# A two-layer decoder step: one chain for both heads, the inverse's last step on two tiles, conditioning by transposes, a new order

## Chip, cores and metric

The kernel runs on one core of one Trainium2 chip. The metric is the device time of one execution in microseconds (us), lower is better; the median of three runs is given. A profile is one execution recorded on the chip.

## The reference, cut to what matters

One inference step of two layers, for a prompt of 512 tokens and for 8 samples of 8 new tokens each (with 1024 cached tokens), D = 1024. All is float32.

```python
def modulate(x, gain, shift, scale):
    return rms_norm(x, gain) * (1 + scale[:, None, :]) + shift[:, None, :]
# layer 0: shift, scale, gate = split(c @ ada_w + ada_b, 3)
proj = modulate(x, ...) @ w_in                  # 1024 -> 6176
q, k, v = causal_conv(qkv), then silu           # 8 q/k heads, 16 v heads of 128
# gated delta rule, chunk by chunk (WY form), per v head
a = tril((k * beta) @ k.T * decay, -1)
t_inv = solve_triangular(eye + a, eye)
u = t_inv @ (v * beta);  w = t_inv @ (k * beta * exp(g))
for each chunk:
    v_new = u - w @ s
    o = (q * exp(g)) @ s + (q @ k.T * decay) @ v_new
    s = s * exp(g_last) + (k * exp(g_last - g)).T @ v_new
o = rms_norm(o) * silu(z);  x = x + gate * (o @ w_out)
# shared k, v = modulate(x, ...) @ w_kv, rms norm and partial rotary on k
# layer 1: differential attention of q over cached and new k, v; silu(z) gate;
#          output projection; x = x + gate * y
```

The conditioning vectors `shift`, `scale`, `gate` come from `c @ ada_w + ada_b` for nine vectors `c`: one of the prompt, eight of the samples.

## The kernel before, in words

All 576 tokens (512 + 64) are held as columns, in two halves of 288; a feature block of 128 is the partition dimension. The big projections split each float32 operand into a high and a low part (`whi`, `wlo`, `hhi`, `hlo`, type fp32r) and sum three products, each 128 x 128 weights by 288 columns. Those are the rows with 128x288 in the profile. Other products are plain fp32, which the profile shows as two records each.

The program has three parts, each written out by a small list scheduler at build time:

- `Opening` loads `x`, the first weights and the first conditioning weights, sums squares, and runs the first products as soon as conditioning arrives (`modulated`).
- `Weave` (the first layer, `phase_a`) keeps a set of generators. Each generator yields the engine it needs next (E or L for TensorE, A for ScalarE (ACT), D or S for VectorE (DVE), P or Q for GpSimd (POOL)), an assumed cost, and the conditions to wait for; then it issues its instructions. `Weave.drive` takes the one that can start first by its own model, and among equals the one of the lowest rank. A `Room` is a buffer that is taken and left. The order that comes out is pinned per engine (`woven`), in the first layer for PE, ACT, DVE and POOL (`PINNED`). Where the model sees TensorE idle for long, it fills in small bf16 products (`fill`). Loads are assumed to land `LATE` after their modelled end.
- `Second` (the second layer, `phase_b`) is a `Weave` too, with SP's queue (most of the loads and stores) pinned as well.

The first layer works on 8 groups `g`, one q/k head and two v heads (`hh` = 0, 1) each. TensorE's projections (`weave_proj`, rank 1000, so they take what the others leave) run ahead of the groups and fill the time between the groups' small steps. Within a group:

- `prep` transposes k and q, scores them, and makes the chunk matrices `ckq`; `decays` makes the decays from `gb`.
- `tinv_dve` and `tinv_pe` invert eight unit triangular 128 x 128 matrices (4 chunks by 2 heads) by blocks of 16, 32 and 64. The last step (64) is two products per matrix, with a scaled copy (`V2`) between them on ACT: block `ck` by `XA` into partitions 64 to 127, then `V2` by the lower right block of `WF` into partitions 0 to 63. The result is `WF`.
- `chain(hh)` runs the state recursion for one head: per chunk `c`, `pk` = k by the state `S` (TensorE), `r0` (DVE), `pw` = `WF` by `r0` (TensorE), `wk` = `pw` times a key scale (ACT), `pk` = `kt` by `wk` (TensorE), new `S` (DVE). `copy_w` copies `pw` plainly to `wv` (ACT) for `outputs`, which computes the chunk's outputs into the bank `po`. Both heads' `pk` and `pw` lie in one PSUM bank, `pc`.
- `output` copies `po` to `ob` and squares it in place, with sums; `post`, `head` and `sample_head` normalize, transpose and gate the output and store it (`ogd`); `gate` makes the gate from the projection with a scratch buffer (`scr`).
- `sample_gdn` and `sample_states` do the same rule for the samples, on POOL, TensorE and DVE.

Conditioning appears in three places (`Opening.modulated`, `ada_units`, `ada_mod`): `c` (32 columns, 9 used) by the weights, on four column tiles of the array at once, leaves four partial sums in four partition groups; a copy to SBUF; then a product with the 0/1 matrix `asel` (9 columns) that transposes and adds the four; then DVE adds the bias into `K.mod`.

Of the kernel before, what the change touches and what calls it, by code (L numbers as in the profile page):

```python
# [18 lines left out]
D = 1024  # L19
# [167 lines left out]
def ada_units(K, W, A):  # L187

    nc = K.nc
    for n, kt in enumerate(K.kts):  # L190
# [4 lines left out]
        for k in range(8):  # L195
# [32 lines left out]


# [3 lines left out]
class Weave:  # L233
# [6 lines left out]
    def __init__(self, K):  # L240
# [3 lines left out]
        self.port = 0.0  # L244
        self.queues, self.coming = {"S": [], "P": []}, []
        self.done, self.live = {}, []
# [5 lines left out]
    def matmul(self, **kw):  # L252
# [57 lines left out]
    def transfers(self, until):  # L310

        while True:
# [13 lines left out]
            else:  # L326
                for q in act:
                    if q[0][0] < 1e-9:
                        name = q.pop(0)[1]
                        self.done[name] = t + (SPARE if "page" in str(name[0]) else LATE), None  # L330
# [20 lines left out]
    def ready(self, w):  # L351

        eng, _, *conds = w[3]
        x, asked = 0.0, {}
        for c in [w[4]] + conds:
            if isinstance(c, Room):
                i = self.taken[c] - self.bufs[c] + asked.get(c, 0)
                asked[c] = asked.get(c, 0) + 1
                c = (0.0, None) if i < 0 else self.left.get((c, i))
            elif isinstance(c, float):  # L360
# [6 lines left out]
            x = max(x, t if e is None else t + ((0.0 if eng in ("E", "L") else 0.06) if eng and e and ENGINE[e] == ENGINE[eng] else PAD if eng in ("E", "L") else HOP))  # L367
        return x

    def drive(self):  # L370
        while self.live:
# [15 lines left out]
            eng, cost, *conds = w[3]  # L387
            pe, idle = eng in ("E", "L"), x - self.free["E"]
# [3 lines left out]
            for c in conds:  # L392
                if isinstance(c, Room):
                    self.took.append((c, self.taken[c]))
                    self.taken[c] += 1
            if pe:
                self.crowd, self.seen = max(0.0, self.crowd - DRAIN * (x - self.seen)), x
            self.advance(w)
            end = x + self.cost, eng
# [11 lines left out]
    def pin(self):  # L411
        woven(self, PINNED)
# [14 lines left out]
class Opening(Weave):  # L427
# [22 lines left out]

    def pin(self):
        woven(self, PINNED + (mybir.EngineType.SP,))
# [112 lines left out]
    def modulated(self, k):  # L565
# [15 lines left out]
        for a in range(2):  # L581
            K.mm(out=ps[:, 256 + 9 * a:265 + 9 * a], lhsT=sb[:, 128 * a:128 * a + 128], rhs=K.asel, start=True, stop=True)
        yield "D", 0.17, ("con", 1)
        v0 = VEC["ada_b"][0] + k
        nc.vector.tensor_add(out=K.mod[:, k:k + 9:8, :], in0=ps[:, 256:274].rearrange("p (a c) -> p a c", a=2),
                             in1=K.vec[:, v0:v0 + 9:8].unsqueeze(2).to_broadcast([128, 2, 9]))
# [264 lines left out]
HOP = 0.2  # L851
LATENCY = 2.3
SHARED = 0.56
LATE = 0.6
TURN = 0.085
# [24 lines left out]
KQS = 2  # L880
# [7 lines left out]
SPARE = 1.4  # L888
# [155 lines left out]
class Group:  # L1044
# [52 lines left out]
    def gate(self, hh, half, ps, room):  # L1097
# [143 lines left out]
    def prep(self):  # L1241
# [53 lines left out]
        W.set("prep1", g)  # L1295
        gbs = self.gbs
# [38 lines left out]

    def q_squares(self, pq, pz, ssk, ssq):
# [23 lines left out]
    def chunks(self):  # L1360
# [20 lines left out]
    def chain(self, hh):  # L1381
# [3 lines left out]
        h = 2 * g + hh  # L1385
        pk, pw = self.pc[:, hh, 0], self.pc[:, hh, 1]
        for c in range(4):
            vr = self.vrs[hh]
            if c:
                S = self.S[c - 1]  # L1390
                yield "E", None
# [1828 lines left out]
```

## Time and profile before

| | |
|---|---|
| median of 3 runs (lowest to highest) | 1145.55 us (1145.44 to 1146.97) |
| the profiled execution's own time | 1145.45 us |
| its span, first to last instruction | 1143.7 us |
| mean granted TensorE clock | 0.996 |
| busy: PE / weight loads / DVE / ACT / POOL | 1118.4 / 1036.8 / 697.5 / 693.5 / 439.7 us |
| DMA moved | 239.97 MB, mean 210 GB/s |
| chain that ended last, share of PE | 78% |

PE is TensorE's matmuls, PEld its weight loads. Ends of matmuls are modelled and overlap, so a matmul's own length (about 0.3 us for 288 columns) is more than the distance to the next one (about 0.13). In the timeline a row is start, length, engine, line, operation, out<-in, shape and count, with the idle time before it and what ended that in brackets. In the groups a row is busy time and mean ns of one, then the engine's idle time before it. In the waits a row is total time waited, number of waits, longest. L271, L285, L1930 and L1935 are the helpers that issue nearly every product and transpose, so tiles tell more than lines.

### The profile page before, as it was taken

The numbers are of one execution on the slowest core, as the hardware profiler recorded it, in microseconds if no ns is written. First come the engines' busy times: TensorE is split into PE (matmuls) and PEld (weight loads), VectorE is DVE, ScalarE is ACT, GpSimd is POOL, SyncE is SP. The second block draws the span as 40 slices with busy tenths as digits, with TensorE's granted clock in tenths as the row PEclk, the third lists the DMA queues.
The fourth block names the chain that finished last, engine by engine and source line by source line (L and its number), as shares of the span: only waits on it lengthen the run. The fifth ranks groups of instructions, "written<-read, shape, count | busy, mean of one in ns | idle before, by whom it ended". The sixth has DMA issues, their size and how long they took to land.

```text
span 1143.7 us, 32504 instructions
## 1 busy us (share of the span) xinstructions
PE 1118.4 (98%) x12651; PEld 1036.8 (91%) x12651; DVE 697.5 (61%) x1803; ACT 693.5 (61%) x1901; POOL 439.7 (38%) x752
## 2 busy tenths in 40 slices
PE   8999999999999999999999999999999999999998
PEld 6899999998989998998989999999998888888998
DVE  4677875777778675876733567565432557556452
ACT  4675877777767877777744424585543566665520
POOL 3443423323334333232223343188972323313341
PEclk9999999999999999999989999999999999999999
DMA  9786565667657575686777698422489988988553
GB/s 363 218 232 168 136 200 142 188 159 193 174 132 192 146 199 149 172 227 159 231 213 192 232 320 299 158 75 75 140 293 328 318 307 304 323 305 288 185 163 95
DMA packets 87644, 239.97 MB, mean 210 GB/s; under 512 B 14451, under 2 KB 28659, under 8 KB 87491
## 3 DMA queue, kind: packets, MB, share of 16 engines
q1 hardware_dynamic: 71938, 181.27, 46.1%
q0 software_dynamic: 15552, 56.63, 22.1%
q8 instruction: 100, 1.64, 0.6%
q14 instruction: 54, 0.43, 0.1%
HBM read 212.02 MB, written 25.84 MB: 208 GB/s over the span
## 4 chain that ended last, share of the span: by engine, by line
PE 78%; ACT 7%; DVE 5%; DMA 4%; issue 3%; POOL 2%; SPq 1%; POOLq 0%; ACTq 0%; DVEq 0%
PE pp L271 24%; PE pp L1930 12%; PE pc L271 7%; PE pq L1930 7%; PE px L1930 4%; PE po L1930 3%; PE pa L271 3%; PE pt L1935 3%; PE pt L271 3%; PE sc L1930 2%; PE pt L1930 2%; PE pv L1930 2%; PE ps L271 2%; DMA whi<-wall 2%; PE pt L285 1%
## 5 line engine op out<-in xcount | busy, mean ns | idle before, releaser
L271 PE MATMUL pp<-hlo,whi 128*128 128x288 f32 x592 | 171.3, 310 | 0.0
L271 PE MATMUL pp<-hhi,whi 128*128 128x288 f32 x592 | 162.7, 295 | 0.0
L2031 POOL TENSOR_TENSOR wlo<-wraw,whi 128x512 fp32r<-128x512 f32 x78 | 106.3, 1376 | 128.7 <-ACT whi L2025 117.1
L1930 PE MATMUL pp<-hhi,whi 128*128 128x288 f32 x432 | 132.9, 308 | 1.1 <-DVE x L1829 0.8
L1930 PE MATMUL pp<-hlo,whi 128*128 128x288 f32 x432 | 127.1, 295 | 0.0
L1930 PE MATMUL pp<-hhi,wlo 128*128 128x288 f32 x432 | 125.6, 295 | 0.0
L271 PE MATMUL pp<-hhi,wraw 128*128 128x288 f32 x576 | 123.7, 298 | 0.0
L271 PEld LDWEIGHTS pp<-hlo,whi 128*128 128x128 f32 x592 | 112.0, 189 | 1.8 <-issue 1.4
L271 PEld LDWEIGHTS pp<-hhi,whi 128*128 128x128 f32 x592 | 112.2, 189 | 0.4
L271 PE MATMUL pp<-hhi,wlo 128*128 128x288 f32 x592 | 104.4, 305 | 0.0
L271 PEld LDWEIGHTS pp<-hhi,wraw 128*128 128x128 f32 x576 | 94.0, 189 | 1.0 <-issue 0.4
L1134 DVE SCALAR_TENSOR_TENSOR y<-u,vec,y 128x600 f32<-128x600 f32 x96 | 80.8, 842 | 9.8 <-ACT y L1131 9.1
L1930 PEld LDWEIGHTS pp<-hhi,whi 128*128 128x128 f32 x432 | 81.4, 188 | 5.4 <-issue 4.6
L271 PEld LDWEIGHTS pp<-hhi,wlo 128*128 128x128 f32 x592 | 85.4, 190 | 0.9 <-issue 0.2
L271 PE MATMUL pp<-hlo,wraw 128*128 128x288 f32 x288 | 84.4, 314 | 0.2 <-DVE hlo L1855 0.2
L1930 PEld LDWEIGHTS pp<-hlo,whi 128*128 128x128 f32 x432 | 81.5, 189 | 0.0
L1930 PEld LDWEIGHTS pp<-hhi,wlo 128*128 128x128 f32 x432 | 80.8, 188 | 0.0
L926 POOL DMA_DIRECT2D wlo<-wall x36 | 32.3, 897 | 119.5 <-ACT wlo L921 78.3
L2490 POOL COPY pg<-ptt 1x1 int32<-1x1 int32 x128 | 27.5, 226 | 124.7 <-PE po L1930 44.8
L2025 ACT CAST whi<-wraw 128x1024 fp32r<-128x1024 f32 x45 | 47.2, 1049 | 42.9 <-PE px L1930 13.1
L1930 PE MATMUL pq<-hhi,whi 128*128 128x288 f32 x200 | 65.0, 325 | 0.6 <-ACT vch L2247 0.4
L1930 PE MATMUL pq<-hhi,wlo 128*128 128x288 f32 x200 | 58.9, 295 | 0.0
(501 smaller groups left out, 3126.9 us busy)
## 6 DMA issues: line engine op xcount, KB each, us to landing
pg<-ck SPq DMA_DIRECT2D x64, 512.0 KB, 5.5
pg<-cv SPq DMA_DIRECT2D x64, 512.0 KB, 5.3
wraw<-wall SPq DMA_DIRECT2D x49, 512.0 KB, 4.1
wraw<-wall POOLq DMA_DIRECT2D x36, 512.0 KB, 5.6
whi<-wall POOLq DMA_DIRECT2D x36, 512.0 KB, 5.5
wlo<-wall POOLq DMA_DIRECT2D x36, 512.0 KB, 5.6
araw<-ada SPq DMA_DIRECT2D x24, 512.0 KB, 4.2
araw<-ada SPq DMA_DIRECT2D x8, 1024.0 KB, 13.7
```

The lines of the kernel that those rows point to most:

```text
L271: return self.K.nc.tensor.matmul(**kw)
L285: return self.K.nc.tensor.transpose(**kw)
L926: K.nc.gpsimd.dma_start(out=lo[:], in_=src, accum_op=ALU.add)
L1134: nc.vector.scalar_tensor_tensor(out=y[:, :YW], in0=u[:, j:j + YW], scalar=cw[j], in1=y[:, :YW], op0=ALU.mult, op1=ALU.add)
L1930: return self.K.nc.tensor.matmul(**kw)
L1935: return self.K.nc.tensor.transpose(**kw)
L2025: nc.scalar.copy(out=hi[:], in_=raw[:])
L2031: (nc.vector if shared else nc.gpsimd).tensor_sub(out=lo[:, q:q + 4], in0=raw[:, q:q + 4], in1=hi[:, q:q + 4].bitcast(F32))
L2490: nc.gpsimd.tensor_copy(out=e, in_=P.ptt[0:1, i:i + 1])
```

## The change

- `chain` serves both heads: one product of k by the state with 256 columns, two DVE steps, two products with `WF`, one ACT copy of 256 columns to `wv`, two products with keys that are scaled ahead (`keys_scaled`, two POOL products of 128x512 per group, `kts`), two DVE steps. `copy_w` is gone. `outputs` does all products of a chunk in one step, after `wv`.
- The inverse's last step puts four of the eight matrices on another tile of the array, alternating: (0,64) with (0,0), then (64,0) with (0,64). A copy `X22` on ACT brings the lower right block to partitions 0 to 63 for the second four, and each copy between is split in two.
- Conditioning: the product with `asel` becomes a transpose of 128x128, and DVE adds the four groups (`grouped`: a reduction and an addition).
- The scheduler knows a `Bank`: TensorE's use waits in its model for the last use by other engines, and theirs for TensorE's. It assumes 0.1 us between engines other than TensorE (`NEAR`), longer landings for some loads (`SLACK`), half the cost for 64x64 products, and passes the cause of a wait on through steps without an engine. SP's queue is pinned in the first layer too.
- `NUDGE` shifts the rank of single steps by hand-written amounts, 260 of them, so that the order of both layers is a new one.
- `output` squares from `ob` into a junk tile and frees `po` after the copy; the gates write the tanh into their own tile; three buffers for the convolution state (`KQS`).
- Before the opening: a memset of `hhi` and eight more warming products.

The diff, cut to its core:

```diff
...
@@ -201,12 +201,19 @@
-        K.mm(out=ps[:, 128:137], lhsT=sb[:], rhs=K.asel, start=True, stop=True)
-        yield "D", 0.22
-        v0 = VEC["ada_b"][0] + kt
-        nc.vector.tensor_scalar(out=K.mod[:, kt, :], in0=ps[:, 128:137], scalar1=K.vec[:, v0:v0 + 1], scalar2=None,
-                                op0=ALU.add)
+        W.transpose(out=ps[:, 128:256], in_=sb[:], identity=K.ident)
+        yield "D", 0.48
+        grouped(K, ps[:, 128:256], kt, 1)
+def grouped(K, ps, kt, n, step=1):
+    nc = K.nc
+    mod = K.mod[:, kt:kt + (n - 1) * step + 1:step, :]
+    nc.vector.tensor_reduce(out=mod, in_=fr(ps[:, 0:1], [[128, n], [1, 9], [32, 4]]), axis=AX.X, op=ALU.add)
+    v0 = VEC["ada_b"][0] + kt
+    nc.vector.tensor_add(out=mod, in0=mod, in1=K.vec[:, v0:v0 + (n - 1) * step + 1:step].unsqueeze(2).to_broadcast([128, n, 9]))
@@ -226,6 +233,74 @@
+class Bank(str):
+    pass
+NUDGE = {
+    "Weave": {("ada_units", 1): -7.3, ("chain", 2): -5.2, ("chain", 3): -4.6, ("chain", 5): 3.9,
...
+}
@@ -260,7 +336,7 @@
-            cost = max(0.116, n * 0.0017)
+            cost = max(0.058, n * 0.00085)
@@ -337,7 +413,9 @@
-        w = [rank, self.n, work, None, (self.now, None)]
+        name = work.__name__
+        self.count[name] = i = self.count.get(name, 0) + 1
+        w = [rank + self.nudge.get((name, i), 0), self.n, work, None, (self.now, None)]
@@ -364,7 +444,13 @@
-            x = max(x, t if e is None else t + ((0.0 if eng in ("E", "L") else 0.06) if eng and e and ENGINE[e] == ENGINE[eng] else PAD if eng in ("E", "L") else HOP))
+            if eng is None:
+                if t + (HOP if e else 0.0) > late:
+                    self.via, late = c, t + (HOP if e else 0.0)
+            elif e:
+                pe, same = eng in ("E", "L"), ENGINE[e] == ENGINE[eng]
+                t += (0.0 if pe else 0.06) if same else PAD if pe else HOP if e in ("E", "L") else NEAR
+            x = max(x, t)
@@ -409,7 +498,7 @@
-        woven(self, PINNED)
+        woven(self, PINNED + (mybir.EngineType.SP,))
@@ -849,9 +933,12 @@
+NEAR = 0.1
+SLACK = {("Second", "kpage"): 1.4, ("Second", "vpage"): 1.4, ("Weave", "st"): 4.5, ("Weave", "x"): 6.0, ("Weave", "cst"): 3.0,
+         ("Weave", "gb"): 2.0, ("Weave", "hi"): 2.0, ("Weave", "w"): 1.0, ("Second", "ada"): 1.5, ("Second", "raw"): 1.4}
@@ -1099,13 +1185,11 @@
-        yield "A", 0.41, Room("scr")
-        sc, = W.took
-        th = scr(K, HT)
-        nc.scalar.activation(out=th[:], in_=ps[:, :HT], func=AF.Tanh, scale=0.5)
+        yield "A", 0.41
+        nc.scalar.activation(out=z[:, sl], in_=ps[:, :HT], func=AF.Tanh, scale=0.5)
-        nc.vector.scalar_tensor_tensor(out=z[:, sl], in0=th[:], scalar=1.0, in1=ps[:, :HT], op0=ALU.add, op1=ALU.mult)
-        W.leave(room, sc)
+        nc.vector.scalar_tensor_tensor(out=z[:, sl], in0=z[:, sl], scalar=1.0, in1=ps[:, :HT], op0=ALU.add, op1=ALU.mult)
+        W.leave(room)
@@ -1293,6 +1377,7 @@
+        W.add(10 * g + 13, self.keys_scaled())
@@ -1333,6 +1418,17 @@
+    def keys_scaled(self):
+        K, A, W, g = self.K, self.A, self.W, self.g
+        for hh in (1, 0):
+            yield "P", 1.4, ("C", g - 1)
+            if hh:
+                self.kts = self.kt, A.kt.tile([128, 4, 128], F32, name="kt1", bufs=1)
+            K.nc.gpsimd.tensor_mul(out=self.kts[hh][:], in0=self.kt[:],
+                                   in1=self.ks[:, 0:4, hh].unsqueeze(2).to_broadcast([128, 4, 128]))
+        W.set("kts", g)
@@ -1367,10 +1463,9 @@
-        for hh in range(2):
-            W.add(10 * g + 17, self.chain(hh))
+        W.add(10 * g + 17, self.chain())
-        yield None, 0, ("S", g, 3, 0), ("S", g, 3, 1), ("wv", g, 3, 0), ("wv", g, 3, 1)
+        yield None, 0, ("S", g, 3), ("wv", g, 3)
@@ -1378,77 +1473,75 @@
-    def chain(self, hh):
...
+    def chain(self):
+        pk, pw = self.pc[:, 0], self.pc[:, 1]
+        bank = Bank("pc")
+            sl = slice(128 * c, 128 * c + 128)
+                yield "E", None, bank
+                W.matmul(out=pk, lhsT=self.kq[0][:, sl], rhs=S[:], start=True, stop=True)
+                r0 = A.ch.tile([128, 2, 128], F32, name="r0")
+                for hh in range(2):
+                    yield "D", 0.34, ("vr", g, hh), bank
+                    h = 2 * g + hh
+                    nc.vector.scalar_tensor_tensor(out=r0[:, hh], in0=pk[:, hh], scalar=A.neg[:, c, h:h + 1],
+                                                   in1=self.vrs[hh][:, c, :], op0=ALU.mult, op1=ALU.add)
+                rs = [r0[:, hh] for hh in range(2)]
-    def copy_w(self, c, hh):
...
+                rs = [v[:, 0, :] for v in self.vrs] if None not in self.vrs else None
+            yield "E", None, bank, *(() if c else (("vr", g, 0), ("vr", g, 1)))
+            rs = rs or [v[:, 0, :] for v in self.vrs]
+            for hh in range(2):
+                W.matmul(out=pw[:, hh], lhsT=self.WF[:, 4 * hh + c, :], rhs=rs[hh], start=True, stop=True)
+            yield "A", 0.38, bank, *((("cqw", g, c - 2),) if c > 1 else ())
+            wv = self.wv[c] = A.ch.tile([128, 2, 128], F32, name="wv", bufs=2)
+            nc.scalar.copy(out=wv[:], in_=pw)
+            W.set("wv", g, c)
+            yield "E", None, ("kts", g), bank
+            for hh in range(2):
+                W.matmul(out=pk[:, hh], lhsT=self.kts[hh][:, c, :], rhs=wv[:, hh], start=True, stop=True)
+            for hh in range(2) if c else (0,):
+                yield "D", 0.35 if c else 0.42, bank, *((("cqw", g, c - 1),) if c else ())
+                if hh == 0:
+                    S2 = A.st.tile([128, 2, 128], F32, name="S")
+                if c:
+                    nc.vector.scalar_tensor_tensor(out=S2[:, hh, :], in0=S[:, hh, :], scalar=self.egl[:, hh, c:c + 1],
+                                                   in1=pk[:, hh], op0=ALU.mult, op1=ALU.add)
+                else:
+                    nc.vector.tensor_copy(out=S2[:], in_=pk)
+            self.S[c] = S2
+            W.set("S", g, c)
+            yield "E", None, ("wv", g, c), Bank("po"), *((("eg", g),) if c == 1 else ()), *((("out", g, c - 2),) if c > 1 else ())
+            for hh in range(2) if c else ():
+                W.matmul(out=po[:, hh, :], lhsT=self.egs[hh][:, 128 * c:128 * c + 128], rhs=self.S[c - 1][:, hh, :],
+                         start=(hh == 0), stop=False)
+                W.matmul(out=po[:, hh, :], lhsT=self.cq[:, 4 * hh + c, :], rhs=self.wv[c][:, hh],
+        yield "A", 0.38, Bank("po")
+        W.set("out", self.g, c)
+            junk = self.A.ch.tile([128, 128], F32, name="junk")
+            nc.scalar.activation(out=junk[:], in_=self.ob[:, c, hh, :], func=AF.Square, accum_out=self.oms[:, c, hh:hh + 1])
+        W.set("oms", self.g, c)
@@ -1494,7 +1587,7 @@
-        yield "S", 0.4, ("O", g), ("gdn", g), ("ssq", g), ("sq", g)
+        yield "S", 0.4, ("O", g), ("gdn", g), ("ssq", g), ("sq", g), *[("oms", g, c) for c in range(4)]
@@ -1662,21 +1755,31 @@
-    yield "L", None, Room("pa"), ("diag", W.diagonals)
+    yield None, 0, ("diag", W.diagonals)
+    yield "A", 0.37
+    X22 = A.ln.tile([64, 4, 64], F32, name="X22")
+    nc.scalar.copy(out=X22[:], in_=WF[64:128, 4:8, 64:128])
+    yield "L", None, Room("pa")
-    for n in range(8):
+    for n in range(4):
-    yield "A", 0.6
-    V2 = A.ln.tile([128, 8, 64], F32, name="V2", tag="V")
-    nc.scalar.activation(out=V2[64:128], in_=pv2[64:128], func=AF.Copy, scale=-1.0)
+        W.matmul(out=pv2[0:64, n, :], lhsT=ck[0:64, 4 + n, 64:128], rhs=XA[0:64, 4 + n, :], start=True, stop=True,
+                 tile_position=(0, 0))
+    V2 = A.ln.tile([128, 4, 64], F32, name="V2", tag="V")
+    for p in (slice(64, 128), slice(0, 64)):
+        yield "A", 0.38
+        nc.scalar.activation(out=V2[p], in_=pv2[p, 0:4], func=AF.Copy, scale=-1.0)
-    for n in range(8):
-        W.matmul(out=pv2[0:64, n, :], lhsT=V2[64:128, n, :], rhs=WF[64:128, n, 64:128], start=True, stop=True,
+    for n in range(4):
+        W.matmul(out=pv2[0:64, 4 + n, :], lhsT=V2[64:128, n, :], rhs=WF[64:128, n, 64:128], start=True, stop=True,
-    yield "A", 0.6
-    nc.scalar.copy(out=WF[0:64, :, 64:128], in_=pv2[0:64])
+        W.matmul(out=pv2[64:128, 4 + n, :], lhsT=V2[0:64, n, :], rhs=X22[:, n, :], start=True, stop=True,
+                 tile_position=(0, 64))
+    for i, p in enumerate((slice(0, 64), slice(64, 128))):
+        yield "A", 0.38
+        nc.scalar.copy(out=WF[0:64, 4 * i:4 * i + 4, 64:128], in_=pv2[p, 4:8])
@@ -3124,6 +3225,9 @@
+                nc.gpsimd.memset(K.hhi[:, 0, 0:512].bitcast(F32), 0.0)
+                for n in (512, 512, 512, 512, 256, 256, 256, 256):
+                    nc.tensor.matmul(out=warm[:, 0:n], lhsT=K.hhi[:, 0, 0:128], rhs=K.hhi[:, 0, 0:n], start=True, stop=True)
...
```

More of the change, by code (lines that the diff above doesn't have):

```diff
@@ L353, in ready @@
         eng, _, *conds = w[3]
-        x, asked = 0.0, {}
+        x, asked, self.via, late = 0.0, {}, (0.0, None), 0.0
         for c in [w[4]] + conds:
@@ L395, in drive @@
                     self.taken[c] += 1
+                elif isinstance(c, Bank):
+                    self.later.append((self.used, (c, eng in ("E", "L"))))
             if pe:
@@ L398, in drive @@
             self.advance(w)
-            end = x + self.cost, eng
+            end = (x + self.cost, eng) if eng else via
             w[4] = end
@@ L581, in modulated @@
         for a in range(2):
[L582 to L586, printed above, removed]
+            self.transpose(out=ps[:, 256 + 128 * a:384 + 128 * a], in_=sb[:, 128 * a:128 * a + 128], identity=K.ident)
+        yield "D", 0.45, ("con", 1)
+        grouped(K, ps[:, 256:512], k, 2, 8)
         self.leave(pt)
@@ L879 @@
 FINE2 = 2
-KQS = 2
+KQS = 3
 ZB = 4
@@ L887 @@
 SB = 3
-SPARE = 1.4
 HALF = 8, 20
@@ L1794, in sample_out @@
     yield "A", 0.46
-    nc.scalar.activation(out=pa[:, 0, :], in_=s.osb[:, 1, :], func=AF.Square, accum_out=s.oms2[:, 0:1])
+    junk = A.ch.tile([128, 128], F32, name="junk")
+    nc.scalar.activation(out=junk[:], in_=s.osb[:, 1, :], func=AF.Square, accum_out=s.oms2[:, 0:1])
     W.set("sq", s.g)
@@ L1970, in drive @@
                     self.taken[c] += 1
+                elif isinstance(c, Bank):
+                    self.later.append((self.used, (c, eng in ("E", "L"))))
             self.advance(w)
-            end = x + self.cost, eng
+            end = (x + self.cost, eng) if eng else via
             w[4] = end
```

138 lines of the change are left out of this document (75 added, 63 removed).

## The prediction

> **What bounds the kernel now.** I read the page first (busy shares, granted clock, chain that ended last), then busy time by stage, then TensorE's timeline, and last the table of waits.
>
> ```profile
> span 1143.7 us, 32504 instructions
> PE 1118.4 (98%) x12651; PEld 1036.8 (91%) x12651; DVE 697.5 (61%) x1803; ACT 693.5 (61%) x1901; POOL 439.7 (38%) x752
> ...
> PE 78%; ACT 7%; DVE 5%; DMA 4%; issue 3%; POOL 2%; SPq 1%; POOLq 0%; ACTq 0%; DVEq 0%
> ```
>
> ```profile
> 46.00:641.00 595.00, 582.64 (x6623) 547.71 (x6622) 410.96 (x1116) 418.59 (x1261) 200.67 (x349) 0.99 0.68 180
> 641.00:1143.70 502.70, 495.21 (x5679) 457.31 (x5677) 261.83 (x624) 253.20 (x596) 220.28 (x343) 1.00 0.68 235
> ```
>
> The second fence is busy time in two stretches, from the opening's end to the first layer's end, and from there on; columns are PE, weight loads, DVE, ACT, POOL, granted clock, DMA share, GB/s. TensorE is busy 98% of either, every other engine at most 70% (418.59 of 595). So what counts is TensorE time: its own work, and what it waits or loses clock. Work moved to DVE, ACT or POOL is free until it delays a TensorE step. The profiled run took 1145.45 us, its span 1143.7; 1.75 lie around it, and the median, 1145.55, is the same within 0.1.
>
> **Inverse's last step.** Two steps a group, eight 64x64 products each, in fp32, so 16 records:
>
> ```profile
> 577.57 1.14 PE L271 MATMUL pa<-XA,ckq 64*64 64x64 f32 x16
> 578.64 0.40 PE L271 MATMUL pp<-hhi,wlo 128*128 128x288 f32 x1
> ...
> 571.59 1.95 PE L271 MATMUL ps<-Ss,kTm 128*32 128x128 f32 x64
> 573.47 0.40 PE L271 MATMUL pp<-hhi,wraw 128*128 128x288 f32 x1
> ...
> 303.43 0.66 PE L285 MATMUL pt<-con_ident,k 128*128 128x128 f32 x4
> 303.84 0.38 PE L271 MATMUL pp<-hlo,whi 128*128 128x288 f32 x1
> ```
>
> Start to start, 16 records take 1.07 us, some 0.13 of it the change of tile shape: 58 ns a record. The change alternates two tiles of the array, which touch different columns. The rows where four column tiles share all 128 rows show what that gives: 64 records in 1.88 us, 29 ns each, though one such record on the whole array takes about 0.10 (four in 0.41). So two tiles should run together: 29 ns a record in place of 58, over 2 steps x 8 groups x 16 = 256 records, 7.4 us less. Bounds: 0 if the tiles take turns, 7.4; I take 7.4, since the nearest row shows overlap. ACT gains a copy (X22) and splits two 0.6 us copies into four of half length, about 0.7 us a group; other projections run meanwhile.
>
> **Conditioning.** 64 products with nine columns become 64 transposes (16 in the opening, 24 in the first layer, 24 in the second):
>
> ```profile
> 22.06 0.53 PE L271 MATMUL pt<-con_ident,adsb 128*128 128x9 f32 x4
> 22.51 0.85 PE L271 MATMUL pt<-araw,cT 128*32 128x256 f32 x12
> ...
> L271 PE MATMUL pa<-con_ident,adsb 128*128 128x9 f32 x48 | 6.8, 215 | 0.0
> L1930 PE MATMUL pt<-con_ident,scr 128*128 128x9 f32 x48 | 6.5, 244 | 0.3 <-ACT scr L2888 0.3
> L2285 DVE TENSOR_REDUCE qss<-scr 128x10 f32<-128x640 f32 x16 | 13.0, 814 | 10.1 <-ACT scr L2281 10.1
> ```
>
> Two products (4 records) take 0.45 us, 0.225 each; four transposes took 0.41, 0.10 each. 48 outside the opening x 0.12 = 5.8 us less. Bounds 0 (if the time goes into waits for DVE) and 5.8; the transposes stand where the products stood, so 5.8. DVE gets a reduction of 36 or 72 elements; from 814 ns for 640, estimated 0.2 to 0.25, 44 times, some 10 us on an engine 69% busy. Hidden by the projections; uncovered, it would be 10.
>
> **One chain for both heads.** Per chunk and head ACT now makes a scaled copy and a plain one of the same bank; both go, for one copy of 256.
>
> ```profile
> L1404 ACT ACTIVATE wk<-pc,ks 128x128 f32<-128x128 f32 x64 | 22.2, 367 | 24.3 <-PE pc L271 20.5 <-DVE S L1413 1.6 <-DVE r L1395 1.5
> L1423 ACT COPY wv<-pc 128x128 f32<-128x128 f32 x64 | 16.4, 268 | 11.9 <-PE pc L271 9.0 <-DVE S L1413 1.1 <-DVE r L1395 0.8
> L1413 DVE SCALAR_TENSOR_TENSOR S<-S,egl,pc 128x128 f32<-128x128 f32 x48 | 16.3, 345 | 18.4 <-PE pc L271 8.2 <-ACT wk L1404 4.7 <-ACT wv L1423 3.5
> L1447 ACT COPY ob<-pc 128x256 f32<-128x256 f32 x32 | 12.0, 373 | 21.5 <-PE pc L271 21.3
> L1236 POOL TENSOR_TENSOR eg<-eg,q 128x512 f32<-128x512 f32 x16 | 21.9, 1375 | 11.3 <-ACT eg L1217 5.7 <-ACT egl L1218 5.5
> ...
> PEld pc L271 <- ACT wv L1423: 5.9, 15, 0.8
> PEld pc L271 <- DVE r L1395: 2.4, 7, 0.5
> PEld pc L271 <- DVE S L1413: 2.4, 6, 0.8
> ```
>
> ACT: 22.2 + 16.4 less, 32 x 0.373 = 11.9 more: 26.7 us less, hidden, so worth nothing by itself. TensorE streams the same columns. What can be gained is its waits. DVE's S waits for ACT's wk and wv, which it does not read: the heads share a bank, and its users exclude each other, which the order was written without knowing. TensorE's weight loads waited 10.7 us on the three commonest of these, the copy off the path leading. Each such wait is partly covered by the matmuls in flight, so the loss lies between 0 and 10.7. By the program the steps on this bank fall from 29 a group to 15. Half of 10.7: 5 us. It can go below nothing too: two DVE steps of 0.35 now follow each other within one chain, and no other head's chain fills the time; projections must. At the worst that costs what it could gain, +10.7.
>
> POOL gets 2 x 1.375 us a group (priced by the equal-sized L1236), 22 us in all. They wait for the previous group's chain, and queued behind them are the weight loads that POOL issues and the `wm` products. Cover:
>
> ```profile
> 138.00:161.00 23.00, 2.95 (x8) 1.00 0.76 226
> 161.00:199.00 38.00, 0.00 (x0) 1.00 0.59 145
> 199.00:221.00 22.00, 2.83 (x8) 1.00 0.70 203
> ```
>
> These are `wk` copies by stretch: 38 us lie between two groups' chains, and POOL is a third busy. Nothing; if uncovered, up to 2.75 x 8 = 22.
>
> **Loads assumed later; queues.** The new slack table puts ACT's work on weights 1.4 us later after their landing than before (2.0 for 0.6). One such load now costs most:
>
> ```profile
> 572.44 9.35 DMA wraw<-wall
> 581.82 1.06 ACT wraw L921
> ...
> 583.93 1.92 PE L271 MATMUL pa<-WF,V 64*64 64x64 f32 x16 [1.84 <-ACT V L1673]
> ...
> 577.00:584.00 7.00, 5.16 (x46) 1.00 0.97 351
> 584.00:591.00 7.00, 7.00 (x38) 0.51 0.88 215
> 591.00:598.00 7.00, 6.62 (x48) 1.00 0.09 31
> ```
>
> ACT stands before a late load, the inverse's copy stands behind ACT, TensorE idles 1.84 us, and then the granted clock is 0.51 for 7 us, which is 7 x 0.49 = 3.4 more. Together 5.2. Bounds: 0, if another load is late, and 5.2; I take 4. The Trainium skill (TensorE: Matmul & The Clock Gate, Part 1: The HAM clock gate) has the clock halved after an idle window of about 3.4 us; this trace shows it after 1.84, so the trace disagrees. By that rule of the Trainium skill only the 1.84 would come back with the stall, and the sum would be 2.6 later (4 x 3.4 / 5.2). SP's queue also becomes a written order in this layer; a load behind a late store then waits with it. Priced below.
>
> **Opening.** Eight more warming products and a memset of 128x512 stand ahead of the first sums:
>
> ```profile
> 2.40 3.78 PE L3126 MATMUL ps<-WF 128*128 128x512 f32 x4 [2.40 <-POOL WF L784]
> 5.97 3.53 PE L446 MATMUL ps<-WF 128*128 128x224 bf16 x29
> 9.34 2.34 PE L271 MATMUL pt<-ones,sq 128*128 128x1 f32 x20
> 12.11 1.27 PE L271 MATMUL pt<-ones,sq 128*128 128x1 f32 x10 [0.43 <-DVE sq L520]
> 15.27 1.08 PE L271 MATMUL pt<-araw,cT 128*32 128x256 f32 x8
> ```
>
> Four records of 512 in 3.4 us are 0.85 each; the new ones have 3072 columns at half the passes, 2.6 us at that clock. The fillers already run up to the sums, so the sums start up to 2.5 later, the last by perhaps 1; against that 16 transposes give back 1.9, and a steadier clock up to 1 (8 of the araw products take 1.08 us at 15.27, 12 of them 0.85 at 22.51). Net between -2 and +2.5; I take +0.5.
>
> **The rest.** The gate's tanh into its own tile, squares read from SBUF so that the po bank is free before them, and three `cso` buffers: 0, they only loosen. S's update now waits for the previous chunk's output products; behind it on DVE stand convolution steps, and who waits for those is a group ahead: 0. The new order of both layers shows in no row; the nearest are the waits that the inverse's weight loads have from the present one:
>
> ```profile
> PEld pa L271 <- ACT WF L1660: 3.9, 5, 1.6
> PEld pa L271 <- ACT V L1673: 2.8, 3, 2.1
> ```
>
> All 6.7 gone, or as much again: -6.7 to +6.7, taken as 0.
>
> **Sum.** -7.4 - 5.8 - 5 - 4 + 0.5 = -21.7, span 1122.0, plus 1.75: 1124 us.
>
> **Rivals.**
> 1. *The order gains as well.* Take all of the 10.7 (5.7 more), and 5 to 7 from the order: 1111 to 1113. For: the waits are small and many, 28 in the three rows of the chain. Against: 98% busy leaves little.
> 2. *Tiles that share rows take turns.* The first of the two steps has both tiles on rows 0 to 63. If the second's weights wait for the first's product, 128 records stay at 58 ns: 3.7 back, 1128. Against: the 29 ns of four tiles sharing all rows. The Trainium skill (TensorE: Matmul & The Clock Gate, Part 3: Packing small matmuls) lets a weight load overlap only when its row group differs; by that rule this rival would hold, and the 29 ns row speaks against it.
> 3. *Given back.* The single chain's longer steps or POOL's products delay ACT and DVE in line, and the order costs: 8 to 19 us back, 1132 to 1143.
> 4. *Slower: late loads.* With SP's queue fixed, loads that come late stop TensorE as the one at 572 did, 5.2 each. Without the 4 counted, the change gains 17.7; four such stalls cost 20.8, 1148.6. It decides from the fourth on. For: DMA at 0.68 of its share and one such case already. Against: the longer slack.
>
> **How the numbers follow.** About 0.2% (2.3 us) is what a measurement can tell here. Forecast, 1117 to 1131, with rival 2 inside it: 0.45 and 0.07. Rival 1: 0.15 for 1107 to 1117, 0.03 below. Rival 3: 0.15. Same, 1143 to 1148: 0.05. Rival 4: 0.10. Cut at 1107 and 1143, that leaves 0.18 out. Faster 0.85, same 0.05, slower 0.10.
>
> **What would show it.** Right: 64x64 records at about 29 ns; no 128x9 products; half as many waits of pc weight loads, none on a wv copy of one head; granted clock 1.00 in every stretch from 46 on; the first layer ending near 623. Wrong: a TensorE idle of over 1 us behind a load or a POOL product, a stretch at half clock, or 64x64 records still at 58.

## The result, and the profile after

| | before | changed |
|---|---|---|
| median, us (4 runs each, same chip) | 1145.49 (1144.61 to 1146.97) | 1128.83 (1126.22 to 1130.13) |
| ratio, 95% interval | | 0.985 (0.983 to 0.9871) |
| profiled execution, us | 1145.45 | 1126.22 |

The kernel is 1.5% faster, 16.7 us. The head of the page after:

```profile
span 1124.5 us, 32457 instructions
PE 1098.5 (98%) x12641; PEld 1025.7 (91%) x12641; DVE 702.9 (63%) x1839; ACT 678.2 (60%) x1829; POOL 453.9 (40%) x769
...
PE 88%; DVE 4%; DMA 3%; POOL 2%; issue 1%; ACT 1%; SPq 0%; POOLq 0%; DVEq 0%; ACTq 0%
```

TensorE bounds the kernel still, now with 88% of the chain that ended last. Busy time by stage (opening, first layer, second layer; columns as in the prediction):

```profile
0.00:47.65 47.65, 43.18 (x361) 32.94 (x361) 25.82 (x72) 21.46 (x45) 18.33 (x52) 0.93 0.89 310
47.65:620.50 572.85, 564.84 (x6645) 539.57 (x6642) 416.92 (x1132) 405.24 (x1188) 217.66 (x376) 1.00 0.70 189
620.50:1124.50 504.00, 490.45 (x5640) 453.21 (x5639) 260.14 (x635) 251.50 (x596) 217.87 (x341) 1.00 0.67 232
```

Against the stretches of before, the first layer is 22.2 us shorter (595.0 to 572.85; 19.3 were forecast), the opening 1.7 longer (0.5 forecast), the second layer 1.3 longer, where 2.9 less was forecast. The forecast first layer ends near 623; it ends at 620.

TensorE's timeline shows both pieces of its own work:

```profile
139.07 0.68 PE L347 MATMUL pa<-XA,ckq 64*64 64x64 f32 x16
139.68 0.40 PE L347 MATMUL pp<-hlo,whi 128*128 128x288 f32 x1
...
694.51 0.30 PE L2034 MATMUL pp<-hhi,wlo 128*128 128x288 f32 x1
694.65 0.38 PE L2039 MATMUL pt<-con_ident,scr 128*128 128x128 f32 x2
694.78 0.38 PE L2034 MATMUL pp<-hhi,whi 128*128 128x288 f32 x1
```

Sixteen 64x64 records take 0.61 us from start to the next start (1.07 before), and two closing transposes 0.13. All waits of `pc` weight loads that the table still lists:

```profile
PEld pc L347 <- issue: 2.0, 8, 0.4
PEld pc L347 <- DVE r L1492: 1.9, 2, 1.3
PEld pc L347 <- ACT scr L1224: 0.2, 1, 0.2
PEld pc L347 <- DVE tp L1682: 0.2, 1, 0.2
```

4.3 us, and none on a copy of one head. Before, the three commonest rows were 10.7; with the next four, here, and two of 0.2 each, the table then had 15.4:

```profile
PEld pc L271 <- ACT wk L1404: 1.2, 6, 0.3
PEld pc L271 <- DVE S L1416: 1.1, 4, 0.4
PEld pc L271 <- ACT pc L1450: 1.0, 4, 0.4
PEld pc L271 <- issue: 1.0, 4, 0.4
```

And one group that the prediction did not look at, the filler products that the scheduler puts where its costs foresee an idle TensorE (first row before, second row after):

```profile
L292 PE MATMUL pp<-cT,con_ident 128*128 128x224 bf16 x24 | 2.8, 259 | 2.0 <-DVE v L695 1.0 <-DVE z L1107 1.0
...
L368 PE MATMUL pp<-cT,con_ident 128*128 128x224 bf16 x104 | 12.0, 260 | 1.0 <-DVE v L779 1.0
```

80 more of them, 9 us of TensorE time that computes nothing.

### The profile page after: what moved, and what is told of

It is laid out like the page before. It is cut to its first block, busy times and chain, and to the rows that moved or that the text cites. A ratio compares the mean times of both kernels' runs of the same rounds, so it can differ in the third digit from the quotient of the medians.

```text
span 1124.5 us, 32457 instructions
## 1 busy us (share of the span) xinstructions
PE 1098.5 (98%) x12641; PEld 1025.7 (91%) x12641; DVE 702.9 (63%) x1839; ACT 678.2 (60%) x1829; POOL 453.9 (40%) x769
## 3 DMA queue, kind: packets, MB, share of 16 engines
q0 software_dynamic: 15552, 56.63, 22.2%
## 4 chain that ended last, share of the span: by engine, by line
PE 88%; DVE 4%; DMA 3%; POOL 2%; issue 1%; ACT 1%; SPq 0%; POOLq 0%; DVEq 0%; ACTq 0%
PE pp L347 28%; PE pp L2034 14%; PE pq L2034 7%; PE pc L347 6%; PE px L2034 4%; PE po L2034 4%; PE pa L347 3%; PE sc L2034 3%; PE pt L2039 3%; PE pt L347 3%; PE ps L347 2%; PE pv L2034 2%; PE pt L2034 2%; PE pt L361 2%; PE pp L368 1%
## 5 line engine op out<-in xcount | busy, mean ns | idle before, releaser
L2130 ACT CAST whi<-wraw 128x1024 fp32r<-128x1024 f32 x45 | 47.2, 1048 | 35.7 <-PE px L2034 12.9
L2034 PE MATMUL pq<-hhi,whi 128*128 128x288 f32 x192 | 62.1, 324 | 0.2 <-ACT vch L2350 0.2
L2034 PE MATMUL pq<-hlo,whi 128*128 128x288 f32 x192 | 56.6, 295 | 0.0
```

The costliest lines, as they stand in the source:

```text
L2034: return self.K.nc.tensor.matmul(**kw)
L2130: nc.scalar.copy(out=hi[:], in_=raw[:])
```

## Experiments

Theory, after the result: the gain is TensorE work and waits of the first layer, and the new order sums to about nothing. Rival: the order (the table of rank shifts) carries the gain. Each time below is a median, each ratio is against runs of the kernel before on the same chip. "Again" is the changed kernel repeated, on the chip on which the layers were taken apart.

**The changed kernel again.** No edit.

> The changed kernel as it is, on the same chip as these others, to compare with. 1127 to 1130 us by every theory.

1128.28 us, ratio 0.9832 (0.9804 to 0.9861).

**No rank shifts at all.**

```
-        self.count, self.nudge = {}, NUDGE.get(type(self).__name__, {})
+        self.count, self.nudge = {}, {}
```

> The changed kernel without the table of rank shifts; every other part of the change stays. My theory (the gain is TensorE work and waits, the shifts about 0): 1122 to 1134 us in place of 1129, the first layer at 569 to 580 us in place of 572.9, and the second shorter by 1 to 4 us, since the new stalls at 620, 792 and 1076 belong to the shifted order. Rival A (the shifts carry the gain of the first layer): 1136 us or more, with the first layer 8 us or more longer and many weight-load waits of 0.3 to 2 us back. Rival B (the shifts cost something): 1122 us or less.

1149.99 us, ratio 1.0024 (1.0009 to 1.0038). The whole gain is gone: by the time rival A, and my theory of the order falls. The profile, of its fastest run (1145.63 us), puts the smaller part of the loss into the first layer. Its two layers, cut at the first layer's last product:

```profile
46.65:626.14 579.49, 575.68 (x6759) 549.87 (x6758) 408.74 (x1129) 401.40 (x1181) 220.32 (x374) 1.00 0.71 186
626.14:1143.90 517.76, 497.47 (x5687) 458.00 (x5685) 261.95 (x640) 253.95 (x605) 217.40 (x343) 1.00 0.66 228
```

With the same cuts the changed kernel again has 572.9 and 504.45, the kernel before 595.6 and 503.25. So without the shifts the first layer is 6.6 longer, still 16.1 shorter than before, and the second is 13.3 longer, 3 of which are 31 fillers of the first behind the cut. The next runs take the two layers apart.

**The first layer in plain order.** The shifts of the first layer alone are left out; the second layer starts from the same modelled state, so its order is held.

```
+ NUDGE.get(type(self).__name__, {}) if type(self).__name__ == "Second" else {}
```

> The changed kernel without the rank shifts of the first layer alone; the second layer's order is held as changed. Theory (the shifts are worth 7 us in the first layer, as the stages of the kernel without any shifts say, and the rest of the change about 19): the first layer ends near 622 us in place of 615.5 to 620.5, the second is unchanged, 1134 to 1137 us. Rival (the loss without any shifts is one of the second layer, and the first layer only looked longer through the boundary): 1129 to 1131 us.

1137.92 us, ratio 0.9914 (0.9886 to 0.9942): 9.6 us slower than again, a little over the forecast. (From here to no shifts at all, 1.0024, is another 12.6 us: what the second layer's shifts bring.) The profile of its repetition, from which the runs on the chain start, shows where the time went:

```profile
L368 PE MATMUL pp<-cT,con_ident 128*128 128x224 bf16 x254 | 27.2, 259 | 1.0 <-DVE v L779 1.0
```

254 fillers in place of 104: 15.2 us more filler, though the kernel is only about 10 longer. So in the trace the shifts win by leaving the scheduler fewer foreseen waits to fill. That fillers alone are the cause was not tried.

**The second layer as before**, products, scratch tile and order, under the changed first layer; then the same order with transposes in the places of the products.

```
-    W.transpose(out=ps[:, 256 + 128 * a:384 + 128 * a], in_=sb[:, 128 * a:128 * a + 128], identity=K.ident)
+    K.mm(out=ps[:, 256 + 9 * a:265 + 9 * a], lhsT=sb[:, 128 * a:128 * a + 128], rhs=K.asel, start=True, stop=True)
...
-    z = P.z[:, h, sl]           # tanh into its own tile
+    th = scr(K, HT)             # tanh through a scratch tile
...
+    self.nudge = {}; slack, hops and start of this layer's scheduler as before
```

> The changed kernel with the second layer as it was before: products with nine columns, the tanh through a scratch tile, and the order that the second layer had before, instruction for instruction by engine. Opening and first layer as changed. Theory (the second layer lost what its new order costs; the first layer's gain does not hang on the second): the second layer takes 499 to 503 us from its first product on, as before, in place of 504 to 506, and the time is 2 to 5 us less, 1124 to 1127 us. Rival (the old order only fitted what the old first layer left behind, and stalls come at the boundary and in the pages): 1129 us or more.

> As the kernel with the second layer as before, but with that layer's 24 conditioning pieces closed by transposes and a reduction on DVE, in the places of the products in the order. Theory of the prediction (0.12 us a piece): 2.5 to 2.9 us less than with the products, 1121 to 1125 us. Rival (TensorE's time for these pieces is covered by waits near them for the scaled copies, as the kernel with products everywhere suggests, which was not slower): within 1 us of it.

1124.97 us, ratio 0.9804 (0.9777 to 0.9831), and 1123.56 us, ratio 0.9801 (0.9771 to 0.983): 3.3 and 4.7 us less than again. The intervals overlap; the stage rows decide. The second layer, from the first layer's last product on: before, changed again, old order with products, old order with transposes:

```profile
640.45:1143.70 503.25, 495.76 (x5683) 457.87 (x5681) 262.10 (x625) 253.75 (x597) 220.28 (x343) 1.00 0.68 235
...
619.05:1123.50 504.45, 490.75 (x5643) 453.52 (x5641) 261.43 (x635) 251.98 (x597) 217.84 (x341) 1.00 0.68 232
...
622.97:1126.10 503.13, 493.76 (x5667) 455.72 (x5664) 261.68 (x625) 253.01 (x597) 219.60 (x343) 1.00 0.68 233
...
618.23:1119.50 501.27, 491.09 (x5643) 452.72 (x5641) 263.69 (x637) 252.59 (x597) 219.13 (x343) 1.00 0.68 234
```

The old order takes its 503 again. With transposes it takes 501.27, with TensorE busy 2.67 less and idle 0.8 more: 1.9 of the forecast 2.9 come through. The changed order has the shortest busy time (490.75) and the longest stage: it idles 13.7 us, 2.2 of them in one wait near 1075, where the old one with transposes idles 10.2. Of the 3.2 between these two, 1.7 is clock that the changed kernel lost behind that wait (last section); the other lost none while TensorE worked. So the new order of the second layer, with that clock, gives back what the transposes bring. The kernel with the old order and transposes has the lowest median here, 1123.56 us.

**Two chains again**, on the plain first layer, beside that plain kernel on one chip, and with them two more edits of it: the banks unknown to the scheduler, and the slack of the first layer's loads 0.6 us as before.

```
-  W.add(10 * g + 17, self.chain())         # and keys_scaled, Bank
+  for hh in range(2):
+      W.add(10 * g + 17, self.chain(hh))   # chain, copy_w, outputs of before
```

> The kernel that these three start from, on the same chip: the changed kernel without the first layer's rank shifts, the second layer's order held. 1136 to 1140 us by every theory.

> The kernel with the first layer in plain order (no rank shifts there, 1138 us), with the two chains of before put back: a scaled and a plain copy per head, no scaled keys on POOL, banks unknown to the scheduler. The second layer's order is held. Theory of the prediction (the chain's waits, 5 us): 1141 to 1146 us, with weight loads of pc waiting 8 us or more on ACT's and DVE's steps again. Rival A (the inverse, the conditioning and the late load carry what the first layer gained): within 2 us of the kernel it starts from, which runs beside it. Rival B (the single chain's two DVE steps in line cost more than the exclusion did): 2 us or more faster than that.

Plain: 1136.83 us, ratio 0.992 (0.9899 to 0.9941). Two chains: 1147.14 us, ratio 1.0015 (1.0 to 1.0031). One chain with scaled keys is worth 10.3 us, the end of the range I gave it and twice the 5 I took. The first layer's order is not held here: it is written anew, with 119 fillers (12.9 us busy) for two chains and 254 (27.2) for one, so the 10.3 is the chain together with what the scheduler makes of it. The largest weight-load waits with two chains:

```profile
PEld pc L347 <- ACT wv L1507: 9.6, 24, 1.1
PEld pc L347 <- DVE S L1497: 3.2, 5, 1.2
PEld pc L347 <- issue: 2.6, 11, 0.4
PEld pc L347 <- ACT ob L1531: 2.2, 6, 0.7
PEld pc L347 <- ACT wk L1488: 2.0, 9, 0.3
```

and the first layer up to the second's first product, two chains and one, whole and then the chain's tile alone (the last pair's columns are PE, PEld, DVE, ACT):

```profile
46.47:631.67 585.20, 573.43 (x6641) 538.01 (x6641) 410.55 (x1135) 419.23 (x1270) 206.85 (x360) 1.00 0.69 182
...
45.94:622.78 576.84, 572.08 (x6729) 546.16 (x6729) 408.41 (x1125) 399.42 (x1175) 220.71 (x376) 1.00 0.70 184
...
46.47:631.67 585.20, 94.19 (x576) 75.73 (x576) 35.60 (x112) 48.00 (x163) 1.00 0.69 182
...
45.94:622.78 576.84, 80.10 (x528) 67.76 (x528) 35.41 (x104) 24.53 (x67) 1.00 0.70 184
```

Outside its busy time TensorE stands 11.8 us with two chains, 4.8 with one. The tile's own busy time falls by 14.1 with the same columns streamed. But ends of matmuls are modelled, so the waits say more: all rows of weight loads of `pc` come to 20.8 us with two chains and 2.8 with one, 18.0 less, which covers the 10.3 of the time.

```
-            c = self.used.get((c, eng not in ("E", "L")), (0.0, None))
+            c = 0.0, None
```

> The same plain order of the first layer, with one chain and scaled keys, but the scheduler does not know that users of a bank exclude each other. Theory (knowing the bank brings part of the 5 us, through the order alone): 1 to 4 us slower than the kernel it starts from, with more waits of pc weight loads. Rival (with one chain the steps follow each other anyway): within 1 us of it.

1136.71 us, ratio 0.9923 (0.9901 to 0.9944): 0.1 from the plain kernel. By the profiles TensorE, ACT, DVE and POOL run the same instructions in the same order, so in the plain order knowing the banks changes nothing once there is one chain. Under the shifted order it was not tried.

```
-  ("Weave", "st"): 4.5, ("Weave", "x"): 6.0, ("Weave", "cst"): 3.0, ("Weave", "gb"): 2.0, ("Weave", "hi"): 2.0, ("Weave", "w"): 1.0,
```

> The same plain order of the first layer, with the slack of its loads back to 0.6 us for all. Theory (the longer slack is what keeps ACT from standing before a late load): 2 to 5 us slower than the kernel it starts from, with an idle of TensorE of over 1 us behind a load and a stretch at half clock. Rival (the late load of before was an accident of its order): within 1 us, no such idle.

1134.23 us (1133.18 to 1134.42), ratio 0.9896 (0.9872 to 0.9921), against 1136.42 to 1137.33 of the plain kernel: 2.6 us faster, no run overlapping, so neither theory. An idle of over 1 us and half clock do come, once, though the chain that leads to this idle holds steps of DVE and ACT and no load:

```profile
398.86 0.22 PE L347 MATMUL pa<-WC,V 32*32 32x32 f32 x2 [1.52 <-ACT V L1740]
...
399.50:407.00 7.50, 7.50 (x61) 6.95 (x56) 4.14 (x16) 7.16 (x22) 4.28 (x7) 0.77 0.36 51
...
L368 PE MATMUL pp<-cT,con_ident 128*128 128x224 bf16 x163 | 17.4, 259 | 1.8 <-DVE v L779 1.0 <-DVE z L1190 0.7
```

1.5 idle and 0.23 x 7.5 = 1.7 of clock, 3.2 together; but 91 fillers fewer, 9.8 us. The shorter slack is another order, with its own stalls and its own fillers.

**The inverse's tiles in turn.** Four products of one tile, then four of the other; order, copies and costs held.

```
     for n in range(4):
         W.matmul(out=pv2[64:128, n, :], ..., tile_position=(0, 64))
+    for n in range(4):
         W.matmul(out=pv2[0:64, n, :], ..., tile_position=(0, 0))
```

> The changed kernel with the inverse's two last steps written so that four products of one tile follow each other and then four of the other; the same products, copies and modelled costs. Theory (two tiles run beside each other only when their products alternate): most 64x64 records at 58 ns again, 256 x 27 ns = 7 us back less what the change from one tile to the other still covers, 1134 to 1136 us. Rival (a product on a quarter of the array is shorter for another reason, or the gain is in the waits around the step): records at about 29 ns still, 1128 to 1130 us. Rival 2 of the prediction (tiles that share rows take turns): the first of the two steps does not change, 3 to 4 us back, 1132 to 1133 us.

1130.72 us, ratio 0.9853 (0.983 to 0.9877): 2 above the changed kernel, which intervals of this width do not settle. The trace does. The edit puts back only part of the cost, since consecutive products of the two tiles still meet at the change (the product behind the changed kernel's fifteenth step, then this kernel's first step and its fifteenth, each with the product behind it):

```profile
575.68 0.80 PE L347 MATMUL pp<-hhi,wraw 128*128 128x288 f32 x4
...
138.95 0.96 PE L347 MATMUL pa<-XA,ckq 64*64 64x64 f32 x16
139.84 0.40 PE L347 MATMUL pp<-hlo,whi 128*128 128x288 f32 x1
...
578.16 0.96 PE L347 MATMUL pa<-XA,ckq 64*64 64x64 f32 x16
579.05 0.80 PE L347 MATMUL pp<-hhi,wraw 128*128 128x288 f32 x4
```

A step takes 0.89 in place of 0.61, 0.28 more; fifteen steps, 4.2. From the first step's start to the product behind the fifteenth it is 440.10 us here (138.95 to 579.05) and 436.61 in the changed kernel (139.07 to 575.68): 3.5. With the order held, most of the added TensorE work counts.

**Conditioning closed by products again**, order held.

```
-  W.transpose(out=ps[:, 128:256], in_=sb[:], identity=K.ident)
+  W.turned_sum(ps[:, 128:137], sb[:])    # product with nine columns, counted as a transpose
-  nc.vector.tensor_reduce(out=mod, ...)
```

> The changed kernel with the conditioning closed by products with nine columns, as before, in the places where the transposes stand (the scheduler counts them as transposes), and without DVE's reduction. Theory (0.12 us a piece, 24 pieces in each layer and 16 in the opening): first and second layer 2.9 us longer each, opening up to 2 us longer, 1134 to 1137 us in place of 1129. Rival A (the transposes brought nothing, since the time went into waits): 1128 to 1130 us. Rival B (DVE's reductions are uncovered): faster, 1125 us or less.

1128.76 us, ratio 0.9838 (0.9816 to 0.9861): no difference that the times show. The pages, this kernel and changed again:

```profile
PE 1102.0 (98%) x12705; PEld 1031.3 (92%) x12705; DVE 692.9 (62%) x1795; ACT 679.4 (60%) x1829; POOL 456.1 (41%) x769
...
PE 1098.1 (98%) x12641; PEld 1025.7 (91%) x12641; DVE 704.0 (63%) x1839; ACT 679.3 (60%) x1829; POOL 454.0 (40%) x769
```

TensorE is busy 3.9 us more, in a span 1.3 longer (1124.8 to 1123.5). The times cannot tell, but the stages can. This kernel's two layers, cut as above:

```profile
45.97:619.82 573.85, 568.30 (x6678) 543.13 (x6677) 411.14 (x1110) 406.30 (x1189) 219.50 (x376) 1.00 0.71 189
619.82:1124.80 504.98, 491.75 (x5667) 455.27 (x5665) 258.19 (x623) 252.13 (x597) 218.22 (x341) 1.00 0.68 232
```

Its second layer loses no clock. That of changed again, 504.45, holds 1.7 of lost clock (last section), so 502.7 without: there the products cost 2.2 of the forecast 2.9, under the new order too. In the first layer they cost 1.0 (573.85 to 572.87), no more than lies between the changed kernel's own two profiles (573.7 in the first).

**No warming products.**

```
-  nc.gpsimd.memset(K.hhi[:, 0, 0:512].bitcast(F32), 0.0)
-  for n in (512, 512, 512, 512, 256, 256, 256, 256):
-      nc.tensor.matmul(out=warm[:, 0:n], ...)
```

> The changed kernel without the memset of 128x512 and the eight warming products behind it. My theory (they only push the first sums back): the opening ends 1 to 1.7 us earlier, at 46.0 to 46.6 us, and the time is 1127 to 1128 us in place of 1129. Rival (they hold the granted clock through the opening): the opening stays at 47 to 48 us or gets longer, with more than the present 6.8 us at half clock, and the time is 1129 to 1132 us.

1129.27 us, ratio 0.9844 (0.982 to 0.9867): no difference that the times show. The opening, without them and then changed again, up to the fillers that open the first layer:

```profile
0.00:46.25 46.25, 40.07 (x341) 29.73 (x342) 25.44 (x71) 20.76 (x44) 17.87 (x51) 0.96 0.89 314
...
0.00:46.18 46.18, 41.72 (x348) 31.73 (x349) 25.43 (x71) 20.79 (x44) 18.35 (x52) 0.93 0.90 316
```

By the mark of the expectation, some 1.1 us further on, 46.25 is 47.3: the rival's "stays", and the 47.65 of the first profile is scatter. But the rival's reason does not hold either, the granted clock is no lower without the products (0.96 against 0.93). Without them the chain that ended last runs for 15.87 us of the opening over a load of conditioning weights (`araw`), where in the changed kernel it runs over TensorE's steps, so two limits lie close together there.

## Why the prediction was right or wrong

The total, 1124, and the place, the first layer, were about right. The composition was not. For the first layer I summed, from the trace, the time from each TensorE record's start to the next record's, by the kind of the first, from the fillers that open the layer to its last product (before, and changed again):

| kind | before | changed | difference | forecast |
|---|---|---|---|---|
| 64x64, inverse's last step | 17.9 | 10.0 | -7.9 | -7.4 |
| conditioning's close | 4.3 | 1.3 | -3.0 | -2.9 |
| chain, `pc` | 68.1 | 57.8 | -10.3 | -5 |
| fillers | 2.2 | 10.3 | +8.1 | none |
| projections, with the waits and lost clock behind them | 392.5 | 386.7 | -5.8 | -4 |
| everything else | 110.6 | 106.8 | -3.8 | 0 |
| sum | 595.6 | 572.9 | -22.7 | -19.3 |

**Inverse: right.** 29 ns a record was the forecast, 612 ns for 16 is 38 with the change of shape. Rival 2 is out: in the first of the two steps both tiles take rows 0 to 63, and its 16 records take the same 0.61 as the second's. By the Trainium skill (TensorE: Matmul & The Clock Gate, Part 3: Packing small matmuls) weights load beside a product only in another row group. Taken alone, that has these take turns, at 58 ns; the trace disagrees, at 0.61 us for 16.

**Conditioning: right on TensorE, less in time.** DVE's reductions take 191 and 230 ns, as estimated. But in the second layer 1.9 of 2.9 came through under the old order and, the lost clock set aside, 2.2 under the new one; in the first layer no more than 1.0 is seen.

**Chain: right mechanism, wrong size.** "Half of 10.7: 5 us" took half of three wait rows, as if the other half were covered. All rows together fell from 15.4 to 4.3, by 11.1, and the tile's time from start to start fell by 10.3: most of the waiting was exposed, not half, and the whole 10.7 would have been the better price. (The prediction's 29 and 15 steps a group count TensorE's alone, those of the outputs' bank with them.) POOL's products for the keys stayed hidden, as forecast.

**Late load: right in its place, wrong in what follows.** The idle at 582 went, and the half clock behind it. But a like one stands at the layers' boundary, where a DVE step is late:

```profile
620.25 0.38 PE L347 MATMUL pp<-hhi,wlo 128*128 128x288 f32 x1
622.63 0.40 PE L2034 MATMUL pp<-hlo,whi 128*128 128x288 f32 x1 [2.00 <-DVE hlo L1959]
...
620.00:627.50 7.50, 5.50 (x49) 4.95 (x51) 6.04 (x9) 2.23 (x4) 5.22 (x4) 0.77 0.56 194
```

2.00 idle and 1.7 of clock. My lower bound, "0, if another load is late", had no thought for what else could be late. Nor is the longer slack what helps: without it the plain kernel is faster.

**Opening: too low.** By the first filler of the first layer it ends at 46.18 and 46.57 in the two profiles of the changed kernel, 44.84 before: 1.3 to 1.7 longer, not 0.5. I blamed the warming products; without them it ends at 46.25. The 16 transposes' 1.9 do not appear. What holds it stays open.

**New order: the step that failed.** The term of 0, between -6.7 and +6.7, was bounded by the inverse's waits in the old order. It is no such term. Without the first layer's shifts the kernel is 9.6 us slower, and without the second's too the whole gain is gone (1.0024). The profile without shifts says where: the first layer is 16.1 shorter than before, in spite of 199 more fillers up to the cut, but the second is 14.5 longer, 3 of them fillers, and the opening 1.8. So under the changed scheduler the plain order costs the second layer most of what the first gains; why it is so much worse there was not tried. The shifts bring 6.6 to 10.4 us back in the first layer, by the profiles without them, and some 10 in the second, which all the same stays some 1.5 behind the old order with the same transposes, and 3.2 with the lost clock. I had both halves as rivals (1 and 3). They happened together, and that the total came within 5 us is in part luck: the chain (5) and the other rows of the first layer (6) brought more than I took, while the fillers (8), the second layer (4) and the opening (1) went the other way. The parts do not add up across orders: 10.3 for the chain and 9.6 for the first layer's shifts already exceed the gain.

**Rival 4: no, but its sign came once.** There is no series of late loads. But in every profile of the changed kernel and its variants TensorE idles 1.2 to 2.9 us, once, for the weights `wlo` near 74 (2.05 in the first profile), where before it waited directly for no load longer than 0.2. An idle of over 1 us behind a load was named as a sign of being wrong. The longer slack is not its cause: with the old slack it is 1.6.

Of what would show it: 64x64 records, the missing 128x9 products, the waits of `pc` and the first layer's end came as written. A granted clock of 1.00 everywhere did not come.

## What to carry to other kernels

Where a scheduler writes the order, every changed cost is a new order, and that order is a term as large as the work saved: price it by what the order has moved in such a kernel, not by the waits in one profile, and test each piece with the order held. Count the filler that the scheduler adds with the work that it frees: 9 us of TensorE busy time here was padding. And keep an old order for a stage whose program hardly changes: here that is worth 3 to 5 us by the medians, 3.2 by the stage rows, half of it clock.

## What was not expected of the hardware

The same idle of TensorE is followed by half clock in one execution and not in the next. Two places, the boundary (2.0 us idle) and a wait near 1075 (2.2 us), each in the changed kernel's first profile and then in its second:

```profile
620.00:627.50 7.50, 5.50 (x49) 4.95 (x51) 6.04 (x9) 2.23 (x4) 5.22 (x4) 0.77 0.56 194
...
619.00:626.50 7.50, 5.01 (x61) 4.36 (x60) 6.27 (x10) 2.41 (x5) 5.42 (x4) 1.00 0.55 189
...
1070.00:1085.00 15.00, 12.44 (x95) 11.99 (x94) 4.38 (x10) 0.62 (x1) 1.24 (x2) 1.00 0.35 106
...
1070.00:1085.00 15.00, 12.44 (x82) 11.99 (x81) 4.23 (x10) 0.62 (x1) 1.01 (x1) 0.89 0.26 83
```

0.77 of 7.5 us and 0.89 of 15 are each 1.7 us lost. The wait near 1075 is 2.23 us in eleven profiles of this kernel and its variants, and in seven of them half clock begins near its end, from 0.2 us before to 1.4 after. The idle for `wlo` near 74 is a third place: half clock comes with it in three of thirteen profiles, at 2.1, 2.3 and 2.9 us, and not at 2.6. Several such places fit the nearly 5 us by which runs of one kernel differ (1125.25 to 1129.93 for the changed one); the mean clocks on record for these runs, 0.992 to 0.995, account for about 3 of it. That is why differences of 2 us were read from the traces. What decides each time was not tried.
